# Rounds of a state-space mixer: a second raw-weight buffer and a second buffer for the finished strip of u, in place of one each

## The chip, the cores and the metric

The kernel runs on one core of one Trainium2 chip. The metric is the device time of one execution in microseconds. A profile is one further execution, recorded instruction by instruction; in it, times count from the start of its span. The engines are called PE (matrix multiplication), DVE (vector), ACT (scalar, with activation functions), POOL and SP. SP issues most of the DMAs, POOL some. PEld is the weight load of PE.

## The reference, cut to what matters

Two layers run on a sequence of 1024 tokens of width 1024, all in float32. Layer 0 is a block-diagonal state-space mixer (64 groups of 16 channels, 64 complex states each) with a gate; layer 1 is an attention with forget gates, whose keys and values come from the output of layer 0.

```python
def _s5_mixer(h, w_in, log_dt, A_re, A_im, B_re, B_im, C_re, C_im, D, w_glu, b_glu, w_out):
    u, z = jnp.split(h @ w_in, 2, axis=-1)
    ...
    ug = u.astype(f32).reshape(bsz, L, N_GROUPS, GROUP)
    bu_r = jnp.einsum('blgc,gpc->blgp', ug, bb_r)
    bu_i = jnp.einsum('blgc,gpc->blgp', ug, bb_i)
    ...
    _, _, s_r, s_i = lax.associative_scan(_cplx_combine, (a_r, a_i, bu_r, bu_i), axis=1)
    y = (jnp.einsum('blgp,gcp->blgc', s_r, C_re.astype(f32))
         - jnp.einsum('blgp,gcp->blgc', s_i, C_im.astype(f32)))
    y = y.reshape(bsz, L, SSM_WIDTH) + D.astype(f32) * u.astype(f32)
    y = jax.nn.gelu(y)
    y = y * jax.nn.sigmoid(y @ w_glu.astype(f32) + b_glu.astype(f32))
    y = y * jax.nn.silu(z.astype(f32))
    return y.astype(h.dtype) @ w_out
```

The change touches `h @ w_in` and what runs beside it.

## The kernel before

A product with float32 operands is made of three: each operand is split into a high part, rounded to the type fp32r (`w_hi`, `aH`), and a low part, the rest (`w_lo`, `aL`), and PE sums hi·hi, hi·lo and lo·hi. The in-projection has 16 strips of 128 output columns: strips 0 to 7 are `u`, strips 8 to 15 are `z`. The weights of a strip are one 128x1024 tile of 512 KB: `w_raw` is loaded by SP, ACT copies it to `w_hi` (line 95 of the helper `split`), DVE subtracts to get `w_lo` (line 103), and `w_raw` is then free. `w_hi` and `w_lo` have two buffers each.

The state-space part is done in eight blocks e of eight groups (of 128 channels). The token axis is cut in 128 chunks of 8 tokens. A round of the loop over e at the end of the printed function does:

- `scan(e)`: DVE turns the inputs of the states (`v`, which ACT copies from PE's `vps`) by tables of cosines and sines (`cT`, `sT`) and runs a scan along the chunks (line 718). `swap_halves` (line 612) then moves the upper and lower 64 partitions of the result to each other's place by two DMAs on SP's queue.
- for block e+1: `load_u` (reads `uu` from DRAM, where `u_d` holds finished strips of u), `turn_in` (PE, result `min`, copied by ACT at line 667), `taps` (PE, `pk`, which needs `moa`, part of which ACT copies at line 656), `states_in` (PE, `vps` from `min` and `uu`), `toeplitz` (ACT and eight small DMAs).
- `rotate_cos`, then `split_weights` for the next strip of the in-projection, then `rotate_sin`: DVE turns the result of the scan back (`r` and `sT`, line 218). `rotate_sin` needs the exchanged half.
- `tables(e+1)`, and `states_out(e)`: PE makes `py` from `uu` (line 738) and from `r` (line 739), ACT applies the gelu and stores go out from POOL.

Between these, `unit()` puts a sixth of a strip of the in-projection on PE as filler: the strips 4 to 7 of `u` (`u_strip`) and the eight of `z` (`z_strip`). Strips 0 to 3 were made before the rounds. `u_strip` writes its finished 128x1024 strip into `ut` (ACT, line 406) and stores it to `u_d` (line 409); `z_strip` copies to `ez` (line 423) and stores to `z_d` (line 426). The instructions are held in order by `ve` for DVE (including the two of a split) and `te` for PE: each piece is issued behind the one before. What they leave open, a scheduler orders with a model of time, on all engines and queues. An engine works through its instructions in that order, so a waiting instruction holds all behind it.

`w_raw` has one buffer here (line 781): `split_weights` takes the strip that lies in it, issues the two halves of the split, and only then calls `load_raw` for the next strip, which must wait until DVE has read the buffer. `ut` has one buffer too (line 389). Behind the rounds (from about 291 us) comes the gate of layer 0 with weights `a_w_glu`, loaded by `weight_strip` (line 87) through the same buffer of `wpool`.

Of the kernel before, what the change touches and what calls it, by code (L numbers as in the profile page):

```python
# [12 lines left out]
F32 = mybir.dt.float32  # L13
# [7 lines left out]
P = 128  # L21
D = 1024
KT = D // P
# [4 lines left out]
TC = 8  # L28
NCH = L // TC
# [7 lines left out]
U_FIRST = 4  # L37
# [6 lines left out]
PI_LO = 3.1415925  # L44


def trunk(tc, a, out):
# [3 lines left out]
    with top:  # L51
        cst = top.enter_context(tc.tile_pool(name="cst", bufs=1))
        wpool = top.enter_context(tc.tile_pool(name="wpool", bufs=2))
# [47 lines left out]
        def split(x, hi, lo, h_eng=None, l_eng=None):  # L101
            h = copy_on(h_eng or S, hi, x)
            parts[:] = h, (l_eng or V).tensor_tensor(out=lo, in0=x, in1=hi.bitcast(F32), op=ALU.subtract)
# [103 lines left out]
        with l0:  # L207
            s5 = l0.enter_context(tc.tile_pool(name="s5", bufs=1, reuse_waits="tile"))
# [3 lines left out]
            tmp = x0x.enter_context(tc.tile_pool(name="s5tmp", bufs=1, reuse_waits="tile"))  # L212
# [7 lines left out]
            def mul(o, x, y, eng=V):  # L220
                return tt(o, x, y, ALU.mult, eng)

            def halves(nm, top_v, bot_v):
                t = (tmp if nm[0] == "s" else s5).tile([P, 1], F32, name=nm, tag=nm)
                G.memset(t[0:64], top_v)
                G.memset(t[64:128], bot_v)
                return t

            sg_pm = halves("sg_pm", 1.0, -1.0)
            sg_mp = halves("sg_mp", -1.0, 1.0)  # L230
            ntpi = halves("ntpi", -2 * PI_LO, 2 * PI_LO)
            npi = halves("npi", -PI_LO, PI_LO)
            half = halves("half", 0.5, 0.5)
            nhpi = halves("nhpi", -math.pi / 2, -math.pi / 2)
            hpi = halves("hpi", math.pi / 2, math.pi / 2)
            e32 = float(np.float32(math.e))
            ecorr = (math.e - e32) / e32
            ebase = tmp.tile([P, NG], F32, name="ebase")
# [113 lines left out]
            for k in (4, 5, 6, 7, 0, 1, 2, 3):  # L352
                pool, tag = ((s5, "ut"), (s5, "bbs"), (s5, "x1m"), (s5, "x2m"))[k - 4] if k >= 4 else (xp, "xw")
# [13 lines left out]
            def chunk(w, c, nm, tag=None):  # L367
                ps = (pj0 if tag else pj).tile([P, HL], F32, name=f"{nm}_{c}", tag=tag or "pj")
                return ps, in_part(ps, w, c, range(KT))


            def chunk2(w, c, nm):
                ps = pj.tile([P, HL], F32, name=f"{nm}_{c}", tag="pj")
                for r in range(2):
                    yield ps, in_part(ps, w, c, range(KT // 2 * r, KT // 2 * r + KT // 2))

            def width(c):
                return 512 if c == 0 else 256

            def u_norm(ps, c, pool=None):  # L380
                et = (pool or s5).tile([P, HL], F32, name="et", tag="et", bufs=2 if pool else 3)
                n = width(c)
                V.tensor_tensor(out=et[:, 0:n], in0=ps[:, 0:n], in1=q2[:, TOK[c]:TOK[c] + n], op=ALU.mult)
                return et

            def u_strip(e, w=None, done=(), ets=(), tags=(None,) * 3):
                split_in = w is None
                w = w or next_weights()
                ut = s5.tile([P, TC, NCH], F32, name="ut", tag="ut")
                bi = s5.tile([P, 1], F32, name="bi", tag="bi", bufs=3)  # L390
                for c in (2, 0, 1):
                    et, m = None, None
                    if c < 2 and ets:
                        et = ets[c]
                    else:
                        if split_in:
                            two = chunk2(w, c, f"u{e}")
                            yield next(two)[1]
                            ps, m = next(two)
                        else:  # L400
                            ps, m = (done[c], None) if c < 2 and done else chunk(w, c, f"u{e}", tags[c])
                        if c == 2:
                            V.tensor_copy(out=bi, in_=ps[:, 256:257])
                        et = u_norm(ps, c)
                    n, k0 = width(c), TOK[c] // TC
                    S.activation(ut[:, :, k0:k0 + n // TC].rearrange("p j k -> p k j"),
                                 et[:, 0:n].rearrange("p (k j) -> p k j", j=TC), AF.Identity, bias=bi)
                    if c == 1:
                        Q.dma_start(out=u_d[P * e:P * e + P], in_=ut)
                    yield m  # L410
# [38 lines left out]
            for e in range(U_FIRST):  # L449
                if e == 3:  # L450
                    with tc.issue_after(last_mod.ins):
                        w3 = weight_strip(a["a_w_in"][3], [P, KT, P])
                    w3_parts = [p.ins for p in parts]
                for _ in u_strip(e, *((w01[e], u01[e]) if e < 2 else (w2, (), u2, (None, None, "u0_0")) if e == 2 else
                                      (w3, (), (), ("u1_0", "u1_1", "u0_1")))):
                    pass
# [142 lines left out]
            sb = l0.enter_context(tc.tile_pool(name="sb", bufs=2, reuse_waits="tile"))  # L599
# [93 lines left out]
            def load_u(e, st):  # L693
                st["uu"] = sb.tile([P, 8, NCH], F32, name="uu", tag="uu")
                loaded.append(Q.dma_start(out=st["uu"], in_=u_d[P * e:P * e + P].rearrange("(g c) j k -> (c j) g k", c=GC)).ins)
# [58 lines left out]
            stored = [None] * (KT + 1)  # L754
            loaded, sts, order = [], [{} for _ in range(KT + 2)], [None, None]
            strips = itertools.chain(*[u_strip(e) for e in range(U_FIRST, KT)], *[z_strip(e) for e in range(KT)])

            def behind(i):
                return ExitStack() if order[i] is None else tc.issue_after(order[i])
# [10 lines left out]
            def unit(n=1):  # L770
                for _ in range(n):
                    te(lambda: next(strips, order[1]))
# [3 lines left out]
            in_w, raws = [], {}  # L776

            def load_raw(e):
                if e < 2 * KT:
                    raws[e] = wpool.tile([P, KT, P], F32, name="w_raw", tag="w_raw", bufs=1)  # L780
                    wdma.append(Q.dma_start(out=raws[e], in_=a["a_w_in"][e]).ins)

            def split_weights():
                if not raws or in_w:
                    return
                e, raw = raws.popitem()
                hi = wpool.tile([P, KT, P], F32R, name="w_hi", tag="w_hi")
                lo = wpool.tile([P, KT, P], F32R, name="w_lo", tag="w_lo")
                with behind(0):
                    split(raw, hi, lo)  # L790
                order[0] = parts[1].ins
                in_w.append((hi, lo))
                load_raw(e + 1)

            def next_weights():
                split_weights()
                return in_w.pop(0)

            load_raw(U_FIRST)
            load_u(0, sts[0])  # L800
            unit(4)
            ve(mat_in, 0, 0, sts[0])
# [16 lines left out]
            for e in range(KT):  # L819
# [4 lines left out]
                if more:  # L824
# [10 lines left out]
                    toeplitz(e + 1, b_)  # L835
                ve(rotate_cos, a_)
                split_weights()
                ve(rotate_sin, a_)
                if more:
# [28 lines left out]
            for k in range(KT):  # L868
                pool, tag = ((s5, "bb"), (s5, "bbs"), (s5, "x1m"), (s5, "x2m"), (sbm, "min_"), (s5, "ut"), (sb, "uu"), (sb, "uu"))[k]
# [595 lines left out]
```

## Time and profile before

| | |
|---|---|
| time, median of 3 runs | 1167.85 us (1165.87 to 1168.64) |
| the profiled execution's own time | 1167.33 us |
| its span in the profile | 1165.3 us |
| PE busy | 1140.4 us, 98% |
| DVE busy | 837.6 us, 72% |
| ACT busy | 607.6 us, 52% |
| POOL busy | 359.7 us, 31% |
| rounds | about 64 to 291 us of the span |

The span goes from the first to the last recorded instruction; 2.0 us of the execution's time lie around it. A row of the timeline gives start, duration, engine, line, operation, output and inputs, and in brackets the idle time ahead of it on its engine and what ended that. "L781 SPq" is the issue of a DMA on SP's queue. In the table of stretches, the digits behind the engines' busy times are PE's granted clock as a share of full speed, the mean busy share of the DMA engines and GB/s. In a row of waits stand the engine, the tile and line that waited, for whom, the total in us, how often, and the longest.

### The profile page before, as it was taken

Reading aid. Unit: us, or ns where it says so; the run is one execution under the profiler, and the core shown is the slowest. Engines: PE = TensorE matmul, PEld = TensorE weight load, DVE = VectorE, ACT = ScalarE, POOL = GpSimd, SP = SyncE. Lnnn points to the kernel's source line nnn. Section 1 sums busy time; section 2 is a strip of 40 time slices with the busy share of each in tenths; the row PEclk is TensorE's granted clock in tenths of the full one; section 3 lists DMA queues with packets and bytes.
Section 4 is the critical chain, followed back from the end, with each engine's and each line's share of the span. In section 5 each row is a group of like instructions: output and inputs, shape, how many; then the busy total and the mean of one; then the engine's idle time right before and its main releaser. Section 6 shows DMA issues by size and latency. Waiting matters only on the chain.

```text
span 1165.3 us, 20641 instructions
## 1 busy us (share of the span) xinstructions
PE 1140.4 (98%) x7506; PEld 1017.1 (87%) x7506; DVE 837.6 (72%) x1735; ACT 607.6 (52%) x1152; POOL 359.7 (31%) x597
## 2 busy tenths in 40 slices
PE   9999998999999999999999999999999999999998
PEld 7688887989888887999999999988988898887886
DVE  7868998986788875935767754358888888898431
ACT  6565685675534333422232443247777777787210
POOL 2300212223000143211344354435455554544100
PEclk9999998999999999999999999999999999999999
DMA  9664566667876773158854349236556464741152
GB/s 360 216 187 120 139 168 156 170 165 260 305 261 210 266 285 112 73 187 267 299 169 152 114 143 270 91 127 147 116 121 142 114 132 106 158 98 64 54 173 72
DMA packets 95108, 197.10 MB, mean 169 GB/s; under 512 B 17728, under 2 KB 43008, under 8 KB 93472
## 3 DMA queue, kind: packets, MB, share of 16 engines
q1 hardware_dynamic: 86176, 170.24, 48.9%
q0 software_dynamic: 8208, 24.45, 6.8%
q10 hardware_dynamic: 624, 1.10, 0.4%
q8 instruction: 59, 0.97, 0.3%
q14 instruction: 41, 0.34, 0.1%
HBM read 138.21 MB, written 46.27 MB: 158 GB/s over the span
## 4 chain that ended last, share of the span: by engine, by line
PE 76%; ACT 8%; DVE 8%; DMA 5%; issue 3%; SPq 1%; POOL 0%; ACTq 0%; DVEq 0%
PE tkps L1022 23%; PE pj_g L114 8%; PE pj_o L114 8%; PE zb L114 6%; PE u L269 4%; PE pj_f L114 4%; PE z L269 4%; PE tp L1272 4%; PE f L114 3%; PE ov L1278 2%; PE ov L1279 2%; PE sp L1239 2%; PE sp L1240 2%; ACT pr L1247 2%; DMA w_raw<-a_w_in 2%
## 5 line engine op out<-in xcount | busy, mean ns | idle before, releaser
L1022 PE MATMUL tkps<-wvh,aH 128*128 128x256 f32 (+1 forms) x768 | 217.9, 285 | 1.4 <-DVE hnt L1051 1.4
L1022 PE MATMUL tkps<-wvh,aL 128*128 128x256 f32 (+1 forms) x768 | 215.1, 281 | 0.0
L1022 PE MATMUL tkps<-wvl,aH 128*128 128x256 f32 (+1 forms) x768 | 215.1, 281 | 0.0
L1022 PEld LDWEIGHTS tkps<-wvh,aH 128*128 128x128 f32 x768 | 144.2, 188 | 2.4 <-issue 1.7
L1022 PEld LDWEIGHTS tkps<-wvl,aH 128*128 128x128 f32 x768 | 144.5, 188 | 0.4 <-issue 0.2
L1022 PEld LDWEIGHTS tkps<-wvh,aL 128*128 128x128 f32 x768 | 144.1, 188 | 0.2 <-issue 0.2
L1249 POOL TENSOR_SCALAR pr<-pr,sm 128x128 f32<-128x128 f32 (+7 forms) x128 | 95.8, 754 | 91.2 <-DVE sm L1248 91.1
L1274 ACT ACTIVATE pth<-tp 128x512 fp32r<-128x512 f32 (+1 forms) x192 | 86.9, 489 | 50.4 <-PE ov L1278 29.5
L1247 ACT ACTIVATE pr<-pr,mx 128x128 f32<-128x128 f32 (+7 forms) x128 | 98.9, 774 | 25.0 <-DVE mx L1244 24.1
L1275 DVE TENSOR_TENSOR ptl<-tp,pth 128x512 fp32r<-128x512 f32 (+1 forms) x192 | 101.1, 552 | 10.0 <-ACT pth L1274 8.9
L95 ACT ACTIVATE w_hi<-w_raw 128x1024 fp32r<-128x1024 f32 x47 | 49.7, 1057 | 83.6 <-PE pj_f L114 20.1
L1244 DVE CUSTOM_DVE_ANT_0 pr<-sp,msk 128x512 f32<-128x512 f32 (+3 forms) x128 | 72.6, 570 | 21.2 <-PE tp L1272 15.5
L1272 PE MATMUL tp<-ident,pr 128*128 128x128 f32 x576 | 82.1, 273 | 2.6 <-DVE ptl L1275 2.6
L1278 PE MATMUL ov<-pth,vhl 128*128 128x256 f32 x320 | 84.0, 296 | 0.3
L1279 PE MATMUL ov<-ptl,vhl 128*128 128x256 f32 x320 | 79.6, 283 | 0.2
L1046 ACT ACTIVATE hsq<-tkps 128x256 f32<-128x256 f32 x64 | 24.6, 385 | 105.1 <-PE tkps L1022 102.5
L1272 PEld LDWEIGHTS tp<-ident,pr 128*128 128x128 f32 x576 | 68.6, 140 | 12.3 <-DVE ptl L1275 2.1
L1049 POOL TENSOR_TENSOR hms<-hms,nhalf 128x4 f32<-128x4 f32 x64 | 70.7, 1105 | 5.4
L1239 PE MATMUL sp<-kk,qs 128*128 128x256 f32 (+2 forms) x192 | 69.9, 367 | 0.6 <-DVE mx L1244 0.5
L1240 PE MATMUL sp<-kk,q 66*128 66x256 f32 (+2 forms) x192 | 65.6, 345 | 0.0
L1051 DVE TENSOR_TENSOR hnt<-tkps,hms 128x256 f32<-128x256 f32 x64 | 27.1, 423 | 51.6 <-POOL hms L1049 51.4
L269 PE MATMUL z<-aH,w_hi 128*128 128x258 f32 (+2 forms) x192 | 62.8, 327 | 0.5 <-ACT ez L423 0.5
(367 smaller groups left out, 3175.6 us busy)
## 6 DMA issues: line engine op xcount, KB each, us to landing
modw<-modw SPq DMA_DIRECT2D x48, 512.0 KB
wvr<-kvq_w SPq DMA_DIRECT2D x12, 1024.0 KB
w_raw<-a_w_in SPq DMA_DIRECT2D x16, 512.0 KB
v_d<-vt POOLq DMA_DIRECT2D x32, 256.0 KB, 3.9
kk<-k_d SPq DMA_DIRECT2D x16, 512.0 KB
vhl<-v_d SPq DMA_DIRECT2D x16, 512.0 KB
qs<-q_d SPq DMA_DIRECT2D x32, 256.0 KB
w_raw<-a_w_out SPq DMA_DIRECT2D x10, 512.0 KB
```

Of the source, the lines that this page charges most:

```text
L114: m = T.matmul(ps, w[wt][:, k, :], act[at][k][half], start=(k == k0 and n == 0), stop=(k == k1 and n == 2)).ins
L269: m = T.matmul(ps[:, 0:c1 - c0], w[wt][:, k, :], act[at][k][i][:, c0:c1], start=(k == 0 and n == 0), stop=(k == KT - 1 and n == 2)).ins
L1022: last_tk[:] = [T.matmul(ps[:, 0:nv], at, wt[:, k, 0:nv], start=(n == 0), stop=(n == 3 * KT - 1)).ins]
L1239: T.matmul(sp[:, 0:wm_], qsl, kk[:, 0, lo:lo + wm_], start=True, stop=False)
L1240: sp_end.append(T.matmul(sp[:, 0:wm_], q1_[:, P * i:P * i + P], kk[0:HD + 2, 1, lo:lo + wm_], start=False, stop=True).ins)
L1247: S.activation(pr[:, 0:nk], pr[:, 0:nk], AF.Exp, scale=-1.0, bias=mx, accum_out=sm)
L1249: G.tensor_scalar(out=pr[:, 0:nk], in0=pr[:, 0:nk], scalar1=sm, scalar2=0.0, op0=ALU.mult, op1=ALU.add)
L1272: T.transpose(out=tp[:, b, :], in_=prs[qi][:, P * (b0 + b):P * (b0 + b) + P], identity=ident)
L1274: S.activation(pth[:, 0:m, dst], tp[:, 0:m, :], AF.Copy)
L1275: V.tensor_tensor(out=ptl[:, 0:m, dst], in0=tp[:, 0:m, :], in1=pth[:, 0:m, dst].bitcast(F32), op=ALU.subtract)
L1278: T.matmul(ov, vhl[:, b, :], pth[:, b - b0, :], start=(b == 0), stop=False)
L1279: end = T.matmul(ov, vhl[:, b, :], ptl[:, b - b0, :], start=False, stop=(b == nb - 1)).ins
```

## The change

Raw weights of odd strips get a buffer of their own in the pool `sb`; those of even strips stay in `wpool`. Two loads are issued ahead of the rounds, and each split then issues the load of the strip after next. The finished strip `ut` of the odd ones of strips 4 to 7 gets a buffer in `sb` as well. Five constants of one value per partition, which had a tile each, become columns of one tile `hv`; `sg_pm` and `sg_mp` stay in the pool `tmp`. The computation is the same.

```diff
+            hv = s5.tile([P, 8], F32, name="hv")
+
+            def halves(nm, top_v, bot_v, at=None):
+                t = tmp.tile([P, 1], F32, name=nm, tag=nm) if at is None else hv[:, at:at + 1]
...
-            ntpi = halves("ntpi", -2 * PI_LO, 2 * PI_LO)
+            ntpi = halves("ntpi", -2 * PI_LO, 2 * PI_LO, 0)
...
-                ut = s5.tile([P, TC, NCH], F32, name="ut", tag="ut")
+                ut = (sb if split_in and e % 2 else s5).tile([P, TC, NCH], F32, name="ut", tag="ut", bufs=1)
...
             def load_raw(e):
                 if e < 2 * KT:
-                    raws[e] = wpool.tile([P, KT, P], F32, name="w_raw", tag="w_raw", bufs=1)
+                    raws[e] = (sb if e % 2 else wpool).tile([P, KT, P], F32, name="w_raw", tag="w_raw", bufs=1)
                     wdma.append(Q.dma_start(out=raws[e], in_=a["a_w_in"][e]).ins)
...
-                e, raw = raws.popitem()
+                e = min(raws)
+                raw = raws.pop(e)
...
-                load_raw(e + 1)
+                load_raw(e + 2)
...
             load_raw(U_FIRST)
+            load_raw(U_FIRST + 1)
```

The order of PE's instructions is the same in both kernels, and DVE's is the same up to the end of the rounds. On SP's queue, at the start of the rounds, the rows before are these (`w_raw_960` is strip 4, `w_raw_968` strip 5, `w_raw_1101` strip 6):

```order
L781 DMA w_raw_960<-a_w_in 128x1024
L409 DMA u_d_91<-ut_606 128x1024
L781 DMA w_raw_968<-a_w_in 128x1024
L409 DMA u_d_91<-ut_644 128x1024
L409 DMA u_d_91<-ut_682 128x1024
L695 DMA uu_962<-u_d_91 128x8x128
L695 DMA uu_1263<-u_d_91 128x8x128
L409 DMA u_d_91<-ut_722 128x1024
L781 DMA w_raw_1101<-a_w_in 128x1024
L409 DMA u_d_91<-ut_970 128x1024
```

And these of the change (`w_raw_956` is strip 4, `w_raw_966` strip 6, `w_raw_958` strip 5, `w_raw_1099` strip 7):

```order
L783 DMA w_raw_956<-a_w_in 128x1024
L411 DMA u_d_91<-ut_602 128x1024
L783 DMA w_raw_966<-a_w_in 128x1024
L411 DMA u_d_91<-ut_640 128x1024
L411 DMA u_d_91<-ut_678 128x1024
L783 DMA w_raw_958<-a_w_in 128x1024
L697 DMA uu_960<-u_d_91 128x8x128
L697 DMA uu_1261<-u_d_91 128x8x128
L411 DMA u_d_91<-ut_718 128x1024
L783 DMA w_raw_1099<-a_w_in 128x1024
L411 DMA u_d_91<-ut_968 128x1024
```

Strip 6 stands where strip 5 stood, strip 7 where strip 6 stood, and strip 5's load has come in ahead of the two `uu`. All later loads of strips of the in-projection likewise stand in the place of the strip before.

On ACT, around the copy `w_hi` of strip 11 (`ez` is strip 9's result, `min` and `v` belong to the next block of the state-space part), before:

```order
L423 ACTIVATE ez0_1929<-z1_0_1968 128x64x8
L423 ACTIVATE ez1_1930<-z1_1_2009 128x32x8
L667 ACTIVATE min__1914<-pin_2042 128x512
L640 ACTIVATE wm_2156<-bb_912 128x64
L95 ACTIVATE w_hi_2109<-w_raw_2052 128x1024
L704 ACTIVATE v1_2069<-vps_2071 128x512
```

and of the change:

```order
L425 ACTIVATE ez0_1927<-z1_0_1966 128x64x8
L95 ACTIVATE w_hi_2107<-w_raw_1870 128x1024
L425 ACTIVATE ez1_1928<-z1_1_2007 128x32x8
L669 ACTIVATE min__1912<-pin_2040 128x512
L642 ACTIVATE wm_2154<-bb_908 128x64
L706 ACTIVATE v1_2067<-vps_2069 128x512
```

The copy has moved three instructions forward, from behind `min` to ahead of `ez1`. The copies of strips 6, 7 and 10 have moved forward in the same way, that of strip 5 back.

On SP's queue at the start of the gate's stage, before (`a_w_glu` are the gate's weights, here the third and the fourth strip's, `b_wz`, `modw` and the reads `zt`, `yt` other data of that stage):

```order
L909 DMA zt_3274<-z_d 128x512
L87 DMA w_raw<-a_w_glu 128x1024 x2
L426 DMA z_d<-ez_2983 128x512
L87 DMA w_raw<-b_wz 128x1024
L912 DMA yt_3266<-y_d 128x1024
L152 DMA modw<-modw 128x1024
L909 DMA zt_3287<-z_d 128x512
L152 DMA modw<-modw 128x1024
```

and of the change:

```order
L428 DMA z_d<-ez_2979 128x512
L87 DMA w_raw<-b_wz 128x1024
L913 DMA zt_3270<-z_d 128x512
L916 DMA yt_3262<-y_d 128x1024
L152 DMA modw<-modw 128x1024
L913 DMA zt_3283<-z_d 128x512
L152 DMA modw<-modw 128x1024
L87 DMA w_raw<-a_w_glu 128x1024 x2
```

The two loads of the gate's weights stood ahead of these rows and stand behind them now; the first gate strip's load has moved forward, into the rounds.

More of the change, by code (lines that the diff above doesn't have):

```diff
@@ L221, in mul @@
                 return tt(o, x, y, ALU.mult, eng)
-            def halves(nm, top_v, bot_v):
-                t = (tmp if nm[0] == "s" else s5).tile([P, 1], F32, name=nm, tag=nm)
+            hv = s5.tile([P, 8], F32, name="hv")
+            def halves(nm, top_v, bot_v, at=None):
+                t = tmp.tile([P, 1], F32, name=nm, tag=nm) if at is None else hv[:, at:at + 1]
                 G.memset(t[0:64], top_v)
@@ L230, in trunk @@
             sg_mp = halves("sg_mp", -1.0, 1.0)
-            ntpi = halves("ntpi", -2 * PI_LO, 2 * PI_LO)
[L232 to L235, printed above, removed]
+            ntpi = halves("ntpi", -2 * PI_LO, 2 * PI_LO, 0)
+            npi = halves("npi", -PI_LO, PI_LO, 1)
+            half = halves("half", 0.5, 0.5, 2)
+            nhpi = halves("nhpi", -math.pi / 2, -math.pi / 2, 3)
+            hpi = halves("hpi", math.pi / 2, math.pi / 2, 4)
             e32 = float(np.float32(math.e))
```

## Prediction

> **What bounds the kernel now.** I read the busy times by stretch first, then the waits inside the rounds (64 to 291 us, the only part that the edits touch, apart from the loads behind it), then the chain through the largest wait. The stretches, with the matmul engine's (PE) granted clock:
>
> ```profile
> core 0: us, PE busy (x) PEld busy (x) DVE busy (x) ACT busy (x) POOL busy (x), PEclk, DMA share, GB/s
> 64.00:291.00 227.00, 216.89 (x1565) 195.62 (x1564) 186.68 (x245) 148.72 (x229) 43.93 (x83) 0.98 0.62 172
> ...
> 186.00:212.00 26.00, 21.47 (x148) 19.78 (x148) 22.23 (x27) 17.02 (x26) 5.28 (x10) 0.87 0.59 139
> ...
> 291.00:380.00 89.00, 89.00 (x384) 71.87 (x383) 73.54 (x114) 42.99 (x63) 0.00 (x0) 1.00 0.75 257
> ```
>
> PE is the bound: in the rounds it idles 227.00 − 216.89 = 10.1 us, and behind them not at all. So an edit here can win some 10 us of idle time and what the lowered clock (0.98 on the mean) costs, nothing more. The waits of 60 to 291 us (total, times, longest) say whom PE waits for:
>
> ```profile
> PE py L739 <- DVE r L218: 5.7, 3, 4.5
> PE pk L678 <- ACT moa L656: 2.6, 1, 2.6
> PE u L269 <- DVE w_lo L103: 1.1, 1, 1.1
> ```
>
> The scalar engine (ACT) makes `w_hi` from the raw weights, the vector engine (DVE) `w_lo`. A second raw buffer is worth something only where a wait for raw weights reaches PE. It does in the chain of waits around the 4.5:
>
> ```profile
> 179.38 1.14 DVE w_lo L103
> 180.54 5.51 DMA w_raw<-a_w_in
> 186.08 1.06 ACT w_hi L95
> ...
> 188.31 1.23 DVE sT L218
> 189.56 1.24 DVE r L218
> 190.84 0.79 PE py L739 x2
> ```
>
> The load of strip 11's weights (strips by their index into the weights) starts when DVE has read strip 10's out of the one buffer, takes 5.51 us, and DVE, whose order is fixed, does that split ahead of the rotation `sT`, `r` that PE needs.
>
> **Term 3, the wait of 4.53.** With two buffers strip 11's load is issued after the split of strip 9, one strip (18 us) earlier:
>
> ```profile
> 162.70 0.38 SPq L781 DMA_DIRECT2D w_raw<-a_w_in  x1
> ...
> 177.69 1.14 SPq L612 DMA_DIRECT2D v<-v  x2
> ```
>
> 162.70 is the issue of strip 10's load, which is now strip 11's: landed 5.5 us later, by 169. So `w_hi` of strip 11 waits only for its own buffer, which PE reads until it ends strip 9. That is where ACT's next copy of a strip's result runs:
>
> ```profile
> 181.45 0.65 ACT L423 ACTIVATE ez<-z 128x256 f32<-128x256 f32 x1 [1.69 <-PE z L269]
> 181.89 0.64 ACT L667 ACTIVATE min__1914<-pin 128x512 f32<-128x512 f32 x1
> ```
>
> `w_hi` now stands right there and takes 1.06, so it ends at about 182.5, and `ez` and `min` behind it run 1.06 later. PE then finds `min` late:
>
> ```profile
> 183.14 1.95 PE L703 MATMUL vps<-uu,min__1914 128*128 128x128 f32 x16
> ```
>
> `min` would end at 181.89 + 0.64 + 1.06 = 183.6: a new wait of 0.5. On DVE:
>
> ```profile
> 175.37 2.29 DVE L718 TENSOR_TENSOR_SCAN v<-dT,r 128x1024 f32<-128x1024 f32 x1
> ...
> 182.36 1.22 DVE L218 TENSOR_TENSOR r<-cT,v 128x1024 f32<-128x1024 f32 x1
> ```
>
> Split 11 follows at 183.5 and ends at 184.7; `sT` also needs the swapped half of the scan `v`, moved by the exchange issued at 177.69. What an exchange takes shows one round earlier, where DVE waited for it alone:
>
> ```profile
> 153.22 2.29 DVE L718 TENSOR_TENSOR_SCAN v<-dT,r 128x1024 f32<-128x1024 f32 x1
> ...
> 162.99 1.23 DVE L218 TENSOR_TENSOR sT<-sT,v 128x1024 f32<-128x1024 f32 x1 [1.57 <-DMA v<-v]
> ```
>
> Scan end 155.5 to 162.99 is 7.5; from 177.66 that gives 185.1 at the latest. So `sT` starts at 184.7 to 185.1, `r` ends 2.5 later, and `py` starts at about 187.3 instead of 190.84. **Gain 3.5**; between nothing (the exchange as late as the load was) and 4.5 (no wait left).
>
> **Terms 1 and 2, the waits of 1.1 and 2.6.** In ACT's and DVE's rows before the second:
>
> ```profile
> 93.21 1.06 ACT L95 ACTIVATE w_hi<-w_raw 128x1024 fp32r<-128x1024 f32 x1 [0.82 <-DMA w_raw<-a_w_in]
> ...
> 113.09 1.06 ACT L95 ACTIVATE w_hi<-w_raw 128x1024 fp32r<-128x1024 f32 x1 [4.03 <-DMA w_raw<-a_w_in]
> ...
> 117.30 0.60 ACT L704 ACTIVATE v<-vps 128x512 f32<-128x512 f32 x1 [1.47 <-PE vps L703]
> ...
> 118.44 1.20 ACT L406 ACTIVATE ut<-et,bi 128x512 f32<-128x512 f32 x1 [0.54 <-DVE et L383]
> ...
> 129.50 0.40 ACT L656 ACTIVATE moa<-x1m 128x64 f32<-128x64 f32 x2
> ```
>
> ```profile
> 114.18 1.23 DVE L103 TENSOR_TENSOR w_lo<-w_raw,w_hi 128x1024 fp32r<-128x1024 f32 x1 [1.40 <-ACT w_hi L95]
> ```
>
> Strip 6's `w_hi` (93.21) loses a wait of 0.82, but ACT's next copy waits for PE anyway; of PE's 1.1 I take **0.3** (bounds 0 and 1.1). Strip 7's `w_hi` (113.09) moves ahead of its 4.03 wait. From 117.30 ACT works almost without a gap to 129.50, where `moa` releases PE. That chain starts with PE's `vps`, so it can shorten only by the 0.54 that it waits for `et`, which DVE reaches 1.40 earlier: **0.55**, bounds 0 and 2.6. About 2.05 of the wait stays.
>
> **Term 4, the clock.** The granted clock changes in stretches of 3.41 us:
>
> ```profile
> 106.05:109.47 3.42, 2.28 (x19) 2.08 (x19) 3.39 (x7) 0.85 (x2) 0.00 (x0) 1.00 0.57 138
> ...
> 126.53:129.95 3.42, 0.82 (x12) 0.58 (x13) 3.38 (x4) 3.38 (x7) 1.47 (x3) 1.00 0.28 55
> 129.95:133.36 3.41, 3.41 (x22) 3.06 (x17) 1.92 (x3) 2.13 (x4) 2.76 (x6) 0.50 1.01 260
> ...
> 184.56:187.97 3.41, 1.75 (x19) 1.24 (x18) 0.80 (x1) 1.89 (x3) 0.00 (x0) 1.00 0.28 109
> 187.97:191.39 3.42, 0.55 (x2) 0.55 (x3) 3.35 (x4) 2.45 (x6) 1.06 (x2) 0.50 0.44 89
> 191.39:194.80 3.41, 3.41 (x18) 3.41 (x17) 3.34 (x5) 1.15 (x1) 0.00 (x0) 0.50 1.03 260
> ```
>
> 1.14 us of idle time in one stretch left the clock full (the first row); 1.67 and 2.60 halved it for the next. PE worked from 190.84 to 194.80 at half clock: 3.96 × 0.5 = 1.98 lost. With 0.5 + 0.4 idle in place of 4.53 this drop goes: **1.98** (bounds 0 and 1.98). The first drop costs 3.41 × 0.5 = 1.7; 2.05 idle is still above 1.67, so I leave it.
>
> [...]
>
> **Given back.** Behind the faster stretch PE reaches the next `py` 0.85 + 3.5 + 1.98 = 6.3 earlier, and there it already waits:
>
> ```profile
> 196.14 0.69 DVE L218 TENSOR_TENSOR moa<-x1m,pwr 128x512 f32<-128x512 f32 x1 [1.00 <-PE py L739]
> ```
>
> ```profile
> 213.81 0.49 PE L739 MATMUL py<-r,moa 128*128 128x128 f32 x2 [0.25 <-DVE r L218]
> ```
>
> DVE's chain to that `r` gains 0.85 + 3.5 and its 1.00 wait for PE, 5.35: **−1.0** (bounds 0 and −2).
>
> **At nothing.** The five constants keep their memsets. The second `ut` lets ACT write strip 7's result without waiting for a store, but ACT then waits for PE. Loads of raw weights that come earlier stand ahead of `uu` loads on SP's queue (in the order's rows, strip 5's ahead of two `uu`):
>
> ```profile
> 79.25 2.07 SPq L695 DMA_DIRECT2D uu<-u_d  x2
> ```
>
> ```profile
> 92.24 1.95 PE L703 MATMUL vps<-uu,min__1029 128*128 128x128 f32 x16
> ```
>
> Issued by 81.3, they have 10.9 us until PE reads them. Another 5.51 us, a whole load in front, still leaves 5.4, about what a transfer takes: nothing, and 2 us if both share the queues badly. The first gating weights come earlier, where PE has no wait.
>
> **The sum.** 0.3 + 0.55 + 3.5 + 1.98 − 1.0 = 5.3. The profiled execution took 1167.33 (span 1165.3 and 2.0 around it), which gives 1162.0; the median of the runs is 1167.85, which gives 1162.5. I say 1162.2.
>
> **The rivals.**
> - The clock also stays full after 129.8, since 2.05 may not be enough in its stretch (it lies in two if the wait shifts), or terms 1 and 2 come nearer their upper bounds: 1.7 to 4 more, 1158 to 1160.5. Against it: 1.67 was enough. If every idle microsecond and both drops went, 10.1 + 3.7 = 13.8, it would be 1154.
> - The exchange takes the load's place: strips' loads now run beside it, and in the row of 162.99 DVE already waits for it. If it lands 1.5 later, at 186.6, `py` starts at 189, over 1.67 of idle time stays, and the clock drops too: a gain of 2 to 3, 1165. For it: 7.5 us for an exchange against 5.5 for the load. Against it: at 184.56 the queues were only 0.28 busy.
> - Slower: the raw weights of the third gating strip. Before, they were issued here:
>
> ```profile
> 293.93 0.86 SPq L87 DMA_DIRECT2D w_raw<-a_w_glu  x2
> ```
>
> ```profile
> 313.08 1.07 ACT L95 ACTIVATE w_hi<-w_raw 128x1024 fp32r<-128x1024 f32 x1 [2.04 <-PE pj_g L114]
> ```
>
> Now five to six loads stand ahead of them (last place in the order): 512 + 256 + 512 + 512 + 256 + 512 KB and their own 512, 3.15 MB. From 294.8 at the 257 GB/s of 291 to 380 us they land at 307.0. PE ends the second strip at 313.08, so they must land by 313.08 − 1.06 − 1.22 = 310.8. Below 197 GB/s PE waits; below some 133 GB/s it waits 7.6 or more, which eats the whole gain and 2.3 beyond, and the clock falls by another 1.7: 1171. Against it: the measured rate leaves 3.8 us.
> - The change doesn't do what it says: a load that stands one strip earlier in the order still waits for something else. The order's rows show each load ahead by one strip and none behind a new wait; 1167.3.
>
> **How the numbers follow.** A measurement of this kernel tells some 0.2%, 2.3 us, from no change. Forecast 0.50 (0.03 of it within 0.2%), larger gain 0.15, exchange 0.20 (0.08 of it within), slower 0.10, no effect 0.05. So faster 0.74, same 0.16, slower 0.10. The range 1158 to 1167.5 leaves out the slower case and the tail of the larger gain.
>
> **What would show it.** Right: `w_hi` of strip 11 without a wait for `w_raw`, `py`'s longest wait under 1, clock 1.00 in 186 to 212, idle time of the rounds near 6. Wrong: `sT` waiting over 1 for `v`, a new PE wait at `vps` of over 1, a wait of `pj_g` for `w_lo` near 310, or the halved clock still there after a wait under 1.

## The result, and the profile after

| | before | after | ratio, 95% interval |
|---|---|---|---|
| median of the runs beside each other | 1168.84 us (6 runs) | 1163.09 us (6 runs) | 0.995 (0.9937 to 0.9963) |
| the same, taken again later | 1169.26 us (11 runs) | 1162.31 us (6 runs) | 0.9934 (0.9922 to 0.9947) |
| the profiled execution, its own time | 1167.33 us | 1163.33 us | |
| its span | 1165.3 us | 1161.5 us | |

The change is 5.75 us faster in the first comparison and 6.95 in the second; 5.65 were forecast (1162.2 against the median of 1167.85 that was known). One further run of the kernel before, at a granted clock of 0.651, took 1929.38 us and is in none of the figures here. In the changed kernel's traces the lines of the rounds are two higher than before (L739 is L741), those behind the rounds four.

The stretches of the changed kernel, with PE's granted clock behind the busy times of PE, PEld, DVE, ACT and POOL:

```profile
64.00:291.00 227.00, 221.40 (x1591) 198.91 (x1590) 192.28 (x254) 154.94 (x237) 43.76 (x83) 0.99 0.64 176
...
186.00:212.00 26.00, 25.66 (x196) 23.35 (x196) 25.36 (x35) 19.57 (x33) 5.50 (x11) 1.00 0.70 171
...
291.00:380.00 89.00, 87.92 (x379) 70.69 (x378) 69.13 (x107) 38.27 (x57) 0.00 (x0) 1.00 0.74 253
```

PE's idle time from 64 to 291 us fell from 10.1 to 5.6, and from 186 to 212 us PE is now busy 25.66 of 26 us at full clock, where it had 21.47 at 0.87. From 291 to 380 us, where it had not been idle at all, it is now idle for 1.1. The waits of 60 to 291 us (total, times, longest):

```profile
PE pk L680 <- ACT moa L658: 1.9, 1, 1.9
PE py L741 <- DVE r L218: 1.9, 2, 1.0
...
PE u L271 <- DVE w_lo L103: 1.1, 1, 1.1
ACT w_hi L95 <- DMA w_raw<-a_w_in: 1.0, 1, 1.0
```

ACT's wait for raw weights went from 9.2 to 1.0. The wait at py that was 4.53 is 0.84 here (the longest at py is now 1.04, at 164.69), in PE's timeline:

```profile
128.84 0.43 PE L680 MATMUL pk<-moa,bb 128*32 128x128 f32 x8 [1.93 <-ACT moa L658]
...
186.33 0.49 PE L741 MATMUL py<-r,moa 128*128 128x128 f32 x2 [0.84 <-DVE r L218]
```

The chain of work that led to it, in order of time:

```profile
181.53 0.84 DVE r L218
182.37 0.29 issue
182.66 1.22 DVE w_lo L103
183.88 1.15 DVE sT L218
185.03 0.02 issue
185.05 1.24 DVE r L218
186.28 0.04 issue
186.33 0.49 PE py L741 x2
```

No DMA is left in it: where the load of 5.51 us and the wait for `w_hi` stood, DVE's own instructions follow each other. The clock in its stretches of 3.41 us:

```profile
126.09:129.51 3.42, 1.49 (x19) 1.05 (x17) 3.38 (x3) 3.38 (x7) 2.00 (x4) 1.00 0.37 86
129.51:132.92 3.41, 3.41 (x15) 3.27 (x15) 1.96 (x6) 1.65 (x5) 2.22 (x5) 0.50 0.97 254
184.12:187.53 3.41, 2.57 (x26) 2.10 (x25) 3.34 (x3) 2.92 (x6) 1.05 (x2) 1.00 0.78 233
187.53:190.94 3.41, 3.41 (x32) 3.41 (x31) 3.34 (x7) 2.12 (x4) 0.00 (x0) 1.00 0.82 164
1044.28:1047.69 3.41, 2.50 (x14) 1.52 (x13) 3.35 (x10) 2.86 (x6) 0.34 (x2) 1.00 0.00 0
1047.69:1051.10 3.41, 3.41 (x13) 2.93 (x13) 3.35 (x11) 1.94 (x3) 1.07 (x3) 0.50 0.14 33
```

The halved stretch behind the wait at `py` is gone, the one behind the wait at `pk` (1.93 idle) is still there, and there is one at 1047.7 that the profile of before did not have.

Last, a new wait, 190 us behind the place that the change was made for:

```profile
375.16 0.50 PE L114 MATMUL pj_o<-aH,w_lo 128*128 128x512 f32 x1 [1.08 <-DVE w_lo L103]
```

PE waits there for the low part of weights of the out-projection, which DVE made late; a second such wait, of 0.33, follows at 398.54. From the last products of the in-projection (283.8) to the first `ms` behind the out-projection (445.1) the changed kernel took 161.3 us; before, 159.3 (290.5 to 449.8). So of the 6.7 us by which this profile was ahead at 284 us, 2.0 are lost again by 445. That is where the experiments start.

### The profile page after: what moved, and what is told of

Read it like the earlier page. It is cut to its first block, busy times and chain, and to the rows that moved or that the text cites. A ratio compares the mean times of both kernels' runs of the same rounds, so it can differ in the third digit from the quotient of the medians.

```text
span 1161.5 us, 20649 instructions
## 1 busy us (share of the span) xinstructions
PE 1140.0 (98%) x7506; PEld 1016.2 (87%) x7506; DVE 836.6 (72%) x1735; ACT 606.9 (52%) x1152; POOL 358.5 (31%) x597
## 4 chain that ended last, share of the span: by engine, by line
PE 71%; DVE 12%; DMA 7%; ACT 7%; issue 3%; SPq 1%; POOL 0%; DVEq 0%; ACTq 0%
PE tkps L1026 23%; PE u L271 6%; PE zb L114 6%; PE pj_o L114 6%; PE z L271 5%; PE pj_f L114 4%; PE tp L1276 4%; DMA zt<-z_d 3%; PE f L114 3%; PE ov L1282 3%; PE ov L1283 2%; PE sp L1243 2%; PE sp L1244 2%; ACT pr L1251 2%; DVE ptl L1279 1%
```

## The experiments

All times are medians, beside runs of the kernel before on the same chip. "Clock" is the mean of the granted clocks of all timed runs, "gate stage" the stretch just named (last `z` to first `ms`) in the run's one profile.

| kernel | us | ratio to before, 95% interval | clock | PE's wait at pk, at py near 143, at py near 187 | gate stage |
|---|---|---|---|---|---|
| before (63 runs in all) | 1169.25 | | 0.994 | 2.60, -, 4.53 | 159.3 |
| the change, first | 1163.09 | 0.995 (0.9937 to 0.9963) | 0.996 | 1.93, -, 0.84 | 161.3 |
| raw buffer alone | 1160.75 | 0.9926 (0.991 to 0.9942) | 0.998 | 1.97, -, 0.87 | 159.4 |
| constants alone | 1169.55 | 0.9998 (0.9985 to 1.001) | 0.995 | 2.68, -, 4.68 | 161.1 |
| second buffer for strip 11 alone | 1163.43 | 0.9948 (0.9933 to 0.9963) | 0.997 | 2.55, -, 0.84 | 159.3 |
| before, wait at py filled | 1166.39 | 0.9972 (0.9963 to 0.9982) | 0.997 | 2.92, -, 0.70 | 159.3 |
| raw buffer and constants | 1161.41 | 0.9936 (0.9922 to 0.995) | 0.998 | 1.92, -, 0.84 | 159.4 |
| second ut alone | 1169.37 | 1.0005 (0.9993 to 1.0017) | 0.994 | 2.69, -, 4.53 | 159.4 |
| raw buffer, moa on POOL | 1160.97 | 0.9933 (0.9919 to 0.9948) | 0.998 | -, 3.00, 0.50 | 159.4 |
| raw buffer, moa on DVE | 1160.60 | 0.9931 (0.9916 to 0.9946) | 0.998 | -, 3.00, 0.78 | 159.3 |
| the change, again | 1162.31 | 0.9934 (0.9922 to 0.9947) | 0.998 | 1.93, -, 0.85 | 159.5 |
| raw buffer alone, again | 1161.57 | 0.9929 (0.9916 to 0.9941) | 0.998 | 1.96, -, 0.83 | 159.3 |
| the change, moa on POOL, store moved | 1159.46 | 0.9909 (0.9895 to 0.9923) | 0.999 | -, -, 0.79 | 161.6 |
| the same, constants' tile wider | 1157.98 | 0.9899 (0.9883 to 0.9916) | 0.998 | -, -, 0.85 | 159.4 |

**The raw buffer alone.** The two new loads and the buffers by parity, with `ut` and the constants as before:

```diff
-                    raws[e] = wpool.tile([P, KT, P], F32, name="w_raw", tag="w_raw", bufs=1)
+                    raws[e] = (sb if e % 2 else wpool).tile([P, KT, P], F32, name="w_raw", tag="w_raw", bufs=1)
...
-                load_raw(e + 1)
+                load_raw(e + 2)
...
             load_raw(U_FIRST)
+            load_raw(U_FIRST + 1)
```

> The second raw-weight buffer alone; ut and the five constants as before. The order in the gate's stage is then that of the kernel before. Theory A (of the 6.3 us that the profile of the change has won by 267 us, 2.0 are lost between 267 and 451 us because the gate's stage is in another order there): 6.0 to 6.5 us faster than before, the halved clock at 188 to 195 gone, no wait of pj_o for w_lo near 375. Rival B (the gate's stage holds PE up by its loads and its vector work in any order, as soon as PE comes earlier): 4 to 4.7 us faster, like the change, with the waits of pj_o for w_lo still there.

8.5 us faster, more than either expected, with the gate stage in the order and the length of before and no wait at `pj_o`. That spoke for theory A. But its distance to the change, 2.3 us, is from two comparisons that were not made side by side, and the constants alone did not fit.

**The constants alone.**

```diff
+            hv = s5.tile([P, 8], F32, name="hv")
...
-            ntpi = halves("ntpi", -2 * PI_LO, 2 * PI_LO)
+            ntpi = halves("ntpi", -2 * PI_LO, 2 * PI_LO, 0)
...
```

> Only the five constants in one tile; buffers as before. The rounds run in the order of before, the gate's stage in that of the change. The prediction costs this edit at nothing. Theory A: PE comes to the gate's stage no earlier than before, so the new order there has room: 0 within 0.7 us, or up to 2 us slower if the new order is worse by itself. Rival: it makes the time shorter, 1 us or more, and part of the change's gain is its own.

The five constants are what changes the order in the gate's stage: this kernel has the rounds of before, yet DVE's and SP's rows behind them are those of the change. In its profile the wait is there too, among PE's waits of 285 to 460 us:

```profile
PE pj_o L114 <- DVE w_lo L103: 1.2, 1, 1.2
```

and the stage takes 161.1. So in that profile the wait came although PE was no earlier: theory A's "the new order has room" is wrong for it. The median of 12 runs shows no cost all the same; the interval of the ratio (0.9985 to 1.001) leaves room for a cost of 1.2 us at most.

**Strip 11 alone.** The second buffer serves one strip of the twelve:

```diff
+                    raws[e] = (sb if e == 11 else wpool).tile([P, KT, P], F32, name="w_raw", tag="w_raw", bufs=1)
...
+                for n in {9: (10, 11), 10: ()}.get(e, (e + 1,)):
+                    load_raw(n)
```

> One raw buffer as before, and a second one that serves strip 11 alone; ut and constants as before. Theory: terms 3 and 4 (the wait of 4.53 at py and the halved clock behind it) carry nearly all: 5.2 to 5.9 us faster, the wait of 2.6 at pk stays. Rival (each strip's earlier weights give a share): 2 to 4 us faster.

5.8 us faster than before: one load that comes in time is worth most of the gain. The wait at `pk` stays at 2.55. The raw buffer alone, beside the same runs of before, is 2.7 us further ahead (the intervals overlap). The shorter wait at `pk` (1.97) is 0.6 of that; what makes up the rest is not shown, for in the two profiles the last `z` starts at nearly the same time (284.91 here, 285.07 there).

**The wait filled.** The loads are those of before; PE only works while it waits:

```diff
+                    for _ in range(17 if e == 3 and hb == 0 else 0):
+                        T.matmul(py[:, 0, :], mi[:, 0].rearrange("p i c -> p (i c)"), uu[:, 0, :], start=True, stop=True)
```

> The kernel before, with 17 further products of uu and minb (two matmul records of about 0.118 us each, 4.0 us in all) on PE ahead of the py that waits 4.53 us; what they write is overwritten. Nothing comes earlier, PE only works while it waits. Theory (the halved clock of 188 to 195 us comes from the idle time): clock full there, 1.5 to 2.0 us faster than before with all loads and waits as they were. Rival (the clock follows something else, or the 1.98 is given back at the next py): within 0.5 us of before or slower.

The stretches at the same place of this kernel:

```profile
187.44:190.85 3.41, 2.71 (x24) 2.52 (x23) 3.34 (x4) 2.67 (x6) 1.05 (x2) 1.00 0.50 108
190.85:194.26 3.41, 3.41 (x33) 3.41 (x31) 3.34 (x5) 1.20 (x2) 0.00 (x0) 1.00 1.02 243
```

Work that nobody needs makes the kernel 2.9 us faster, more than the 1.5 to 2.0 expected (the interval of the ratio is 2.1 to 4.3 us). The clock stays at 1.00 (before, it was 0.50 from 187.97 to 194.80), and `py` itself comes hardly earlier (190.53, before 190.84; the `py` of the round before was already 0.3 ahead, 165.23 against 165.53). So the halved clock there is a consequence of the idle time, and it is worth some 3 us, about half of what strip 11's load brings.

**The raw buffer and the constants.** The change without the second `ut`; all orders are those of the change.

```diff
-                ut = (sb if split_in and e % 2 else s5).tile([P, TC, NCH], F32, name="ut", tag="ut", bufs=1)
+                ut = s5.tile([P, TC, NCH], F32, name="ut", tag="ut")
```

> The change without the second ut: second raw buffer and the five constants in one tile; every engine and queue has the order of the change. Theory A (the second ut is worth nothing; the constants' tile costs what the change stays behind the raw buffer alone): like the change, 1163 us, about 2 us slower than the raw buffer alone, with pj_o waiting over 1 us for w_lo near 375. Rival (the second ut costs the 2 us, by its place or its stores): like the raw buffer alone, 1161 us.

1161.41 us and a gate stage of 159.4 with the very order of the change: theory A's wait was not there. The rival, that `ut` costs the 2 us, was tried by itself:

**The second ut alone** (the reverse of that edit, on the kernel before).

> The kernel before with the second ut alone; every engine and queue has the order of before. Theory: ACT's wait of 4.2 us for the store of u at 136 us goes, and PE's waits stay as they were: 0 within 0.7 us. Rival (ACT's wait held up what PE waited for): 1 us or more faster.

Nothing, as forecast: 1.0005, with ACT's waits for the store of `ut` down from 11.6 us in five to 6.2 in three. PE's waits did not all stay as they were: at py near 165 us this profile has 1.98, the profile of before 0.93.

**The change again, beside the raw buffer alone.**

> The changed kernel once more, beside the raw buffer alone on one chip, since the run of the raw buffer with the constants has the same orders as the change and yet was 1.7 us below it, with no wait of pj_o for w_lo over 0.3 us. Theory C (that wait and the 1.7 us belong to single executions; the second ut and the constants cost little): 1161 to 1162 us, within 1 us of the raw buffer alone. Theory A (the gate's stage in the new order costs 2 us): 1163 us, 2 us or more behind the raw buffer alone.

> The raw buffer alone once more, for the difference to the run before it: 1160.5 to 1161.5 us by either theory; theory C has it within 1 us of the change, theory A 2 us or more ahead.

0.74 us apart, theory C's side, though the change lies 0.3 above the range given for it; over both runs of each the medians are 1162.4 (12 runs) and 1161.4 (11 runs). This profile of the change had no wait at `pj_o` over 0.3 and a gate stage of 159.5. So with the new order of that stage the 2 us are lost in some executions and not in others: in three of the five profiles that have it (161.3, 161.1, 161.6, but 159.4 and 159.5), and in none of the nine with the order of before (159.3 or 159.4).

The traces show how little room the new order leaves. DVE made the weights for which PE waited at 375.16 here, in the first profile of the change:

```profile
360.44 0.69 DVE L918 TENSOR_TENSOR zt<-zt,q2p 128x512 f32<-128x512 f32 x1 [2.34 <-DMA zt<-z_d]
...
373.89 1.22 DVE L103 TENSOR_TENSOR w_lo<-w_raw,w_hi 128x1024 fp32r<-128x1024 f32 x1
```

and in the second, with PE's use of them:

```profile
357.78 0.69 DVE L918 TENSOR_TENSOR zt<-zt,q2p 128x512 f32<-128x512 f32 x1 [1.79 <-DMA zt<-z_d]
...
371.23 1.22 DVE L103 TENSOR_TENSOR w_lo<-w_raw,w_hi 128x1024 fp32r<-128x1024 f32 x1
...
372.85 0.39 PE L114 MATMUL pj_o<-aH,w_lo 128*128 128x512 f32 x1
```

From its last wait for a read of `zt` to this `w_lo` DVE works without a gap, 13.45 us in both. In the first profile `w_lo` ends (375.11) 1.0 us after PE has become idle, in the second 0.4 before PE uses it; in the kernel before it ended 3.6 ahead (376.99, used at 380.55). From 284 to 400 us DVE waits 15.3, 14.6 and 18.3 us for the reads of `zt` in the three profiles that lost, 13.1 and 12.7 in the other two with the new order, and 5.6 to 11.3 in the nine with the order of before. So the new order has used up most of the lead, and the loss stands in the three profiles in which DVE waits longest for `zt`; why these reads land when they do is not shown.

**The wait at pk.** The largest wait left is 1.9 at `pk`, for ACT's copy of a column of `moa`. Two kernels with the raw buffer alone make that copy elsewhere, one on POOL, as here, the other on DVE (`V` in place of `G`):

```diff
-                S.activation(moa[:, ls, 0], x1m[:, gs], AF.Copy)
+                G.tensor_copy(out=moa[:, ls, 0], in_=x1m[:, gs])
```

> The second raw-weight buffer alone, and the first column of moa (a copy of x1m, two of 128x64 a block) made by POOL in place of ACT. Theory (the wait of 2.0 at pk is for ACT's copy alone, which stands behind 12 us of other ACT work, and the halved clock behind it is that wait's): the wait and the halved stretch at 130 go, 3 to 3.7 us faster than the raw buffer alone, 1157 to 1158 us. Rival (POOL's own queue holds the copy behind stores that wait for ACT): PE waits as long or longer, 1161 us or more.

> As the run before it, with the copy on DVE, ahead of DVE's own part of moa. Theory: the wait at pk and the halved stretch go as well, but DVE has 16 more instructions, some of them ahead of the rotation that PE waits for at 166 and 187: 2 to 3.5 us faster than the raw buffer alone. Rival (DVE's chain is the next bound): PE's waits for r at 166 and 187 grow by as much as the one at pk falls, within 1 us of the raw buffer alone.

Both theories miss. The rivals have the time about right, but not the reason: with the copy on POOL PE does not wait for it, and with the copy on DVE it is not the waits at 166 and 187 that grow. The wait at `pk` is gone in both, and the time is that of the raw buffer alone (1161.4 over both of its runs) within 0.8 us. PE's timeline of the kernel with POOL's copy, 14 us later:

```profile
143.53 0.49 PE L739 MATMUL py<-r,moa 128*128 128x128 f32 x2 [3.00 <-DVE r L218]
```

and DVE's:

```profile
140.52 1.22 DVE L218 TENSOR_TENSOR sT<-sT,v 128x1024 f32<-128x1024 f32 x1 [3.50 <-DMA v<-v]
```

The wait has moved on to the exchange of the scan's halves, the rival that the prediction had put at 185 us. It takes the place of those at `pk` (1.97 with the raw buffer alone) and at py near 166 us (1.09), and it brings a halved stretch as the one at `pk` had:

```profile
140.62:144.03 3.41, 0.50 (x4) 0.50 (x5) 3.38 (x4) 1.65 (x3) 0.00 (x0) 1.00 0.03 10
144.03:147.44 3.41, 3.41 (x18) 3.41 (x18) 3.34 (x5) 3.34 (x7) 1.05 (x2) 0.50 0.57 144
```

The exchange was issued here, on SP's queue:

```profile
131.72 0.33 SPq L409 DMA_DIRECT2D u_d<-ut  x1
132.14 2.33 SPq L612 DMA_DIRECT2D v<-v  x2
```

The scan had ended by 130.8; the exchange stood behind a store of u that itself waited for ACT.

**The store moved.** The change, with `moa`'s column on POOL and the stores of u in the rounds on POOL's queue:

```diff
-                        Q.dma_start(out=u_d[P * e:P * e + P], in_=ut)
+                        (G if split_in else Q).dma_start(out=u_d[P * e:P * e + P], in_=ut)
```

> The change, with the first column of moa on POOL, and the stores of u in the rounds issued by POOL in place of SP, so that the exchange of the scan's halves at 132 us no longer stands on SP's queue behind the store of u. Theory (with the wait at pk gone, PE waits 3.0 us at 143.5 for r, and that for the exchange): the exchange is issued some 1.3 us earlier, PE's wait falls from 3.0 to 1.7 or less, 1 to 2 us faster than the run with moa on POOL if the halved clock goes with it up to 3. Rival (the exchange's time is set by the eight stores of y that run beside it, and u's store joins them on POOL): PE's wait at 143.5 stays 3 us or grows, no gain.

On SP's queue now:

```profile
129.95 1.14 SPq L614 DMA_DIRECT2D v<-v  x2
```

and on DVE, with no wait ahead of it:

```profile
136.02 1.22 DVE L218 TENSOR_TENSOR sT<-sT,v 128x1024 f32<-128x1024 f32 x1
```

Issue to use was 8.4 us, and is at most 6.1. PE's waits at 129 and at 143 are both gone, more than the 1.3 us that was expected, and no stretch of the rounds is halved. Of the expected 1 to 3 us it won 1.5 against the run with `moa` on POOL; the two were not run side by side, their intervals overlap, and this kernel has the second `ut` and the constants as well, so that the waits show the effect better than the times. The gate stage took 161.6, with a wait at `pj_o` once more, this time for a later piece of the weights, which DVE made behind a wait of 3.02 for another load (`rf`):

```profile
394.84 0.50 PE L114 MATMUL pj_o<-aH,w_lo 128*128 128x512 f32 x1 [1.39 <-DVE w_lo L103]
```

**The same with a wider tile.** One number changes, eight columns or 32 bytes per partition more, and the order in the gate's stage is that of the kernel before:

```diff
-            hv = s5.tile([P, 8], F32, name="hv")
+            hv = s5.tile([P, 16], F32, name="hv")
```

> The run with the store of u moved, and the constants' tile 16 columns wide in place of 8. The only effect on the orders is that DVE's and SP's rows in the gate's stage are those of the kernel before again. Theory (the order that the 8 columns bring about costs 0 to 2 us there, by the wait of pj_o for w_lo): no wait of pj_o over 0.5 us, and 0 to 2 us faster than with 8 columns, 1157.5 to 1159.5 us. Rival (the wait comes from PE's being earlier, in any order): the wait of 1.4 us at 395 stays, and the time too.

159.4 in the gate stage, no wait at `pj_o`, and 1157.98 us, 1.5 less (the two were not run side by side, and their intervals overlap). It has the lowest median of all kernels here, 0.9899 of before.

## Why the prediction came out right

The total was right, and the mechanism of the largest term too. That the forecast of 5.65 met the measured 5.75 so closely is luck in part: the profiled execution gained 4.0 (1167.33 to 1163.33) where the sum says 5.3, and two steps failed in opposite directions. Term by term:

- **Term 3, 3.5 us.** Right in place, mechanism and size. Strip 11's weights were there, `w_hi` waited for PE's strip 9 (180.52) and not for a load, the exchange had landed when DVE came to `sT`, and the wait fell from 4.53 to 0.84: 3.7. The extra 0.5 at `vps` did not come: `w_hi` ran in the time that ACT had spent waiting for PE ahead of `ez` (1.69 in the prediction's row), and `min` started at 181.90, as before at 181.89. That this is the change's core is shown by strip 11 alone. Of the signs named, `py`'s longest wait under 1 was missed by little: it is 1.04, at another `py` (164.69).
- **Term 4, 1.98 us.** Right in kind, as the filled wait shows, and too small by the medians, where the filled wait won 2.9 (interval 2.1 to 4.3). In its one profile the last `z` starts 2.0 earlier than before (288.70, before 290.69; 0.3 of it stood ahead of the wait), near the size that was forecast for one execution.
- **Terms 1 and 2, 0.3 and 0.55.** The first was 0 (1.14 to 1.13: ACT's 0.82 did not reach PE), the second 0.67.
- **The first halved stretch, left as it was.** True of the first profile (1.93 idle, 129.51 to 132.92 at 0.50). In the second one of the change the same wait lay across two stretches:

```profile
125.34:128.75 3.41, 1.84 (x16) 1.60 (x14) 3.38 (x4) 3.38 (x4) 0.96 (x2) 1.00 0.31 49
128.75:132.16 3.41, 3.05 (x26) 2.70 (x27) 3.14 (x6) 2.83 (x8) 3.25 (x7) 1.00 0.88 248
```

1.57 and 0.36 idle, and the clock stayed full: the rival given 0.15, by the means that it named.
- **Given back at the next py, 1.0.** This step failed. The wait of 0.25 there went, and `py` came at 207.15, 6.66 earlier than before. The working moved DVE's chain by its wait for PE alone and left the exchange its wait of 1.15; that wait fell to 0.30 in the trace of the change.
- **The constants at nothing.** This step failed too, and in the first profile the two failures partly covered each other: 1.0 was not given back, 2.0 were lost. Merging five tiles into one changes no instruction's work, but with it the order of the gate's stage is another, and in three of five profiles that stage is 2 us longer. The prediction saw the order's rows there and looked for the damage at the loads of the third gating strip (near 310 us; PE had no wait there, and the rival priced at 1171 did not come). It came 65 us later, through DVE, which waited for reads of `zt` and made the out-projection's weights late.
- **The second ut at nothing.** Right.

Open: why the reads of `zt` land later in one execution than in the next, so that the new order costs 2 us or nothing, and why the width of a tile of constants tips the order. The two waits at `pj_o` make 1.4 of the 2.0 in the first profile; the rest was not traced.

## What to carry to other kernels

A second buffer pays where the one load that it brings forward ends a wait of the bounding engine; look for that load first: here it brought 5.8 of the 8.5 us of the whole second buffer. A wait of the bounding engine can cost more than its length: here the clock was halved behind the one at `py`, and the wait merely filled was already worth 2.9 of 5.8 us. When a wait is taken away, read the next one off the trace before counting the gain: here 2 us at `pk` turned into 3 at `py` until the store ahead of the exchange was moved as well. And an edit that touches only the layout of memory can reorder a stage far away, so compare the order of the whole program, not that of the place that was edited.

## What the runs showed of the hardware

The clock does not follow idle time alone. 1.57 us of idle time in one stretch left it full, as above, and behind 1.66 (the kernel before) and 1.93 (the first profile of the change) it was halved; but with the second ut alone it stayed full behind 1.87:

```profile
125.57:128.99 3.42, 1.55 (x14) 1.31 (x12) 3.38 (x5) 3.37 (x5) 0.51 (x1) 1.00 0.21 39
128.99:132.40 3.41, 2.58 (x24) 2.32 (x25) 3.14 (x5) 3.10 (x7) 3.41 (x8) 1.00 0.83 243
```

And in some executions it was halved behind far less idle time: 0.91 at 1044.28 in the first profile of the change, and 0.35 in that of the raw buffer alone, near the start:

```profile
52.56:55.97 3.41, 3.06 (x26) 2.65 (x23) 3.41 (x22) 1.92 (x7) 0.92 (x2) 1.00 0.51 127
55.97:59.39 3.42, 3.42 (x18) 3.42 (x18) 3.35 (x17) 2.86 (x12) 0.08 (x2) 0.50 1.03 230
```

What else decides it is not shown. Each such stretch costs up to 3.41 × 0.5 = 1.7 us (an estimate), and runs of one kernel differ by as much as three of them would make: those of the change lie between 1160.26 us (clock 1.000) and 1165.02 (0.995).

The stretches begin at 126.09 us in one profile of the change and at 125.34 in another. With their borders so placed, the same wait of 1.93 us lay in one stretch and was followed by a halved one, or lay across two (1.57 and 0.36) and was followed by none. In the rows shown here the clock was halved behind stretches with 0.35 to 2.91 us of idle time (the raw buffer alone from 52.56 us, the run with `moa` on POOL from 140.62).
